# First layer's attention as seven staged steps in a written order, with TensorE turning the context's probabilities

## The chip, the cores and the metric

The kernel runs on one core of a Trainium2 chip. The metric is the device time of one execution in microseconds (us): lower is better. A profile is one more execution with the hardware profiler on. TensorE is called PE, VectorE DVE, ScalarE ACT, GpSimd POOL; SP is the engine that issues most DMAs.

## The reference, cut to what matters

Two layers over 2048 latent and 256 context tokens of width 1024. The change lies in the first layer's mixer: windowed attention with 16 query heads in 4 key/value groups, head size 64. A block of 128 latent queries reads its own and the two neighbouring key blocks (masked to a distance of 128) and all 256 context keys, in one softmax that also has a learned sink logit per head. The two context blocks read context keys only. The output is gated and projected.

```python
s_loc = jnp.where(valid, einsum('bqhgd,bkhd->bhgqk', qs, ks) * scale, NEG_INF)
s_ctx = einsum('bqhgd,bkhd->bhgqk', qs, kc) * scale
p = softmax(concatenate([s_loc, s_ctx, sink], axis=-1))
o = einsum('bhgqk,bkhd->bqhgd', p[..., :n_loc], vs) + einsum(..., p[..., n_loc:-1], vc)
y = (o * silu(g)) @ w_o
```

All products are done to about fp32 accuracy by splitting one factor into a high and a low half and adding matmuls.

## The kernel before

Three phases: the first layer's projections (to about 711 us), its attention with the output projection (711 to about 1450 us), and the second layer, which for most of its time is attention too (its dense part from about 1850 us).

The first layer's attention works in 72 units: 18 blocks of 128 tokens by 4 key/value groups, 4 heads each. Units 0 to 7 are context (256 keys), 8 to 11 and 68 to 71 are the outer latent blocks (512 keys), the 56 between have 640 keys and are called wide here. The steps of a unit:

- `score` (L509 to L523): PE makes a head's windowed scores (bank `pS`), DVE adds the mask, takes the maximum and moves them to SBUF (L513); the context scores of two heads share a bank and leave it by two more DVE operations (L523).
- `maxima` (L531 to L538): DVE makes the exponent's bias `nm` out of both maxima and the sink; `expo` (L542): ACT's four exps; `sums` (L547 to L549): the sink's exp, the sum, the reciprocal.
- `halves` (L558 to L562): ACT rounds the probabilities to fp16 (`hl`), POOL subtracts for the low half (L559), two heads at a time, and one DMA transposes all of it: 40 pieces of 128x128 in a wide unit.
- `value` (L573 to L595): ten matmuls into `pV`, the norms spread (`rb`, L579) and turned by PE (L581), the two halves of `pV` brought together by DVE (L585, L589), the gate on POOL (L590), and the split for the output projection (ACT L594, DVE L595).
- `project` (L616 to L623): the output projection in 16 parts per block of tokens, three matmuls of 512 columns each, drawn from the list `rest`.

Tile's scheduler sets the order on every engine from priorities here. The second layer's attention stands in a written order (`manual_schedule`), one `step` per 128 queries of a head: 6 of 18 key blocks are turned by PE (`turn`, L1125), ACT and DVE make their halves (L1132, L1134), and 12 pieces are rounded by ACT (L1113), subtracted by POOL (L1115) and transposed by two DMAs of 12 pieces each.

Of the kernel before, what the change touches and what calls it, by code (L numbers as in the profile page):

```python
# [19 lines left out]
KT = 8  # L20
# [12 lines left out]
def body(ctx: ExitStack, tc: tile.TileContext, x, c, ctxt, c_ctx, norm_g_0, ada_w_0, ada_b_0,  # L33
# [407 lines left out]
    work_2 = mk("a2k", 2)  # L441
    pss_2 = mk("a2ps", 4, space=PSUM)
# [9 lines left out]
    msk = w0p_2.tile([128, 640], F32, name="msk", tag="msk")  # L452
    dma(out=msk, in_=mask)
    vals = {}

    def load_v(t):

        raw = late2_2.tile([128, 4, 64], F32, name="vraw", tag="vraw", bufs=2)
        dma(out=raw.rearrange("p h d -> p (h d)"), in_=vv_d[t])
        if t < NC_:  # L460
            dst = late2_2.tile([128, 4, 128], F16, name=f"vc{t}", tag=f"vc{t}", bufs=1)
        else:
            dst = late2_2.tile([128, 4, 128], F16, name="vt", tag="vt", bufs=6)
# [3 lines left out]
        vals[t] = dst  # L467
# [10 lines left out]
    def load_unit(u):  # L478
# [10 lines left out]
        u["mx"] = small_2.tile([128, 4, 2], F32, name="mx", tag="mx")  # L489
        u["s"] = [None] * 4  # L490
# [4 lines left out]
    def load_gate(u):  # L495
        kv, t = u["kv"], u["t"]
        u["gt"] = late2_2.tile([128, 2, 128], F32, name="gt", tag="gt", bufs=2)
        dma(out=u["gt"], in_=ga_d[t // 3][:, 2 * kv:2 * kv + 2, (t % 3) * 128:(t % 3 + 1) * 128])

    def score(u, g):  # L500
        nw, nk, kv, wt = u["nw"], u["nk"], u["kv"], u["wt"]
        q2, mx = u["q2"], u["mx"]
        if g % 2 == 0:
            u["sp", g // 2] = work_2.tile([128, 2, 640], F32, name="s4", tag="s4", bufs=5)
        s = u["s"][g] = u["sp", g // 2][:, g % 2]
        if nw:
# [3 lines left out]
            PE.matmul(p[:, 0:nw], q2[:, g, :], kw[:, 1, 0:nw], start=False, stop=True)  # L510
            m0 = (wt[0] - u["t"] + 1) * 128
            assert all((wt[i] - u["t"] + 1) % 3 == (m0 // 128 + i) % 3 for i in range(len(wt)))
            V.tensor_tensor_reduce(out=s[:, 0:nw], in0=p[:, 0:nw], in1=msk[:, m0:m0 + nw], op0=ALU.add, op1=ALU.max,  # L513
                                   scale=1.0, scalar=-3e38, accum_out=mx[:, g, 0:1])
        if g % 2:
            p = pss_2.tile([128, 2, 256], F32, name="pS", tag="pS")
            for w in range(2):
                gw = g - 1 + w
                PE.matmul(p[:, w], q2[:, gw, :], kc[:, kv, 0, :], start=True, stop=False)
                PE.matmul(p[:, w], q2[:, gw, :], kc[:, kv, 1, :], start=False, stop=True)  # L520
            for w in range(2):
                gw = g - 1 + w
                V.tensor_scalar(out=u["sp", g // 2][:, w, nw:nk], in0=p[:, w], scalar1=1.0, scalar2=None,  # L523
                                op0=ALU.mult, op1=ALU.max, accum_out=mx[:, gw, 1:2])

    def maxima(u):
        hs = slice(u["kv"] * 4, u["kv"] * 4 + 4)
        mx = u["mx"]
        u["nm"] = nm = small_2.tile([128, 4], F32, name="nm", tag="nm")
        if u["nw"]:  # L530
            V.tensor_tensor(out=nm, in0=mx[:, :, 0], in1=mx[:, :, 1], op=ALU.max)  # L531
            V.tensor_tensor(out=nm, in0=nm, in1=sink8[:, hs], op=ALU.max)
        else:
            V.tensor_tensor(out=nm, in0=mx[:, :, 1], in1=sink8[:, hs], op=ALU.max)
        V.tensor_scalar(out=nm, in0=nm, scalar1=-0.125, scalar2=PS, op0=ALU.mult, op1=ALU.add)  # L535
        u["sm"] = small_2.tile([128, 4], F32, name="sm", tag="sm")
        u["es"] = es_ = small_2.tile([128, 4], F32, name="es", tag="es")
        V.tensor_tensor(out=es_, in0=sink[:, hs], in1=nm, op=ALU.add)  # L538

    def expo(u, g):  # L540
        nk, s = u["nk"], u["s"][g]
        A.activation(out=s[:, 0:nk], in_=s[:, 0:nk], func=AF.Exp, bias=u["nm"][:, g:g + 1],  # L542
                     scale=0.125, accum_out=u["sm"][:, g:g + 1])

    def sums(u):
        sm, es_ = u["sm"], u["es"]
        A.activation(out=es_, in_=es_, func=AF.Exp)  # L547
        V.tensor_tensor(out=sm, in0=sm, in1=es_, op=ALU.add)
        V.reciprocal(out=sm, in_=sm)  # L549

    def halves(u):

        nh = u["nk"]
        hl = mid_2.tile([128, 4 * 2 * 640], F16, name="hl", tag="hl")[:, 0:8 * nh]
        h4 = hl.rearrange("p (g w k) -> p g w k", g=4, w=2)
        for w in range(2):
            gs = slice(2 * w, 2 * w + 2)
            A.copy(out=h4[:, gs, 0], in_=u["sp", w][:, :, 0:nh])  # L558
            G.tensor_tensor(out=h4[:, gs, 1], in0=u["sp", w][:, :, 0:nh], in1=h4[:, gs, 0], op=ALU.subtract)  # L559
        n = nh // 128  # L560
        ht = mid_2.tile([128, 4 * 2 * 5, 128], F16, name="ht", tag="ht")[:, 0:8 * n]
        nc.sync.dma_start_transpose(out=ht, in_=hl)  # L562
        u["ht"] = ht.rearrange("p (g w k) q -> p g w k q", g=4, w=2)

    def value(u, i):
        wt, kv, t = u["wt"], u["kv"], u["t"]
        n = len(wt) + 2
        if i == 0:
            u["acc"] = psv_2.tile([128, 512], F32, name="pV", tag="pV")
        acc = u["acc"]  # L570
        vs = vals[(wt + [0, 1])[i]][:, kv, :]
        ph, pl = [u["ht"][:, :, w, i, :] for w in range(2)]
        PE.matmul(acc, vs, ph, start=(i == 0), stop=False)  # L573
        PE.matmul(acc, vs, pl, start=False, stop=(i == n - 1))
# [26 lines left out]
    def project(t):  # L601
# [3 lines left out]
        def part(nh, k):  # L605
# [18 lines left out]
            if nh == 1:  # L624
                dma(out=x1_d[t], in_=xt)
# [10 lines left out]
    NE = 2  # L636

    def stage(n, i):

        us = units[n] if n < nu else None  # L640
        ue = units[n - 1] if 0 < n <= nu else None
        ux = units[n - 2] if 1 < n <= nu + 1 else None
        uv = units[n - 3] if n > 2 else None
        if i == 0 and n + 1 < nu:
            load_unit(units[n + 1])
        if i == 0 and 2 <= n < nu + 2:
            load_gate(units[n - 2])
        nv = len(uv["wt"]) + 2 if uv else 0
        if ux and i == 0:
            sums(ux)  # L650
            halves(ux)
        if us and i < 4:
            score(us, i)
        if ue and i < 4:
            expo(ue, i)
        if uv and 1 <= i <= nv:
            value(uv, i - 1)
        if us and i == 4:
            maxima(us)
        if rest and 1 <= i <= 4 and (n > 6 or i < 3):  # L660
            with tc.high_priority(offset=-200):
                rest.pop(0)()
        if uv and i == 5:
            uv.clear()

    load_unit(units[0])
# [816 lines left out]
```

## Time and profile before

| what | us |
|---|---|
| three runs | 3612.79, 3618.59, 3619.69 (median 3618.59) |
| profiled execution, its own time | 3625.8 |
| span of that execution in the trace | 3623.9 |
| PE, DVE busy in the span | 3310.2, 2570.0 |
| granted TensorE clock, mean over the span | 0.959 of 2.4 GHz |

Busy times are of the whole span; the stretch in which the change lies has to be looked at by itself. The granted clock is a mean over its two levels, 1.2 and 2.4 GHz. PE's busy time includes the modelled tails of its matmuls, so what a matmul costs is read from one start to the next.

### The profile page before, as it was taken

To read this page: it belongs to the slowest core of one execution; us is meant where nothing else is said; L and a number is where in the kernel's file an instruction comes from. 1 tells how busy PE (TensorE), PEld (TensorE's weight loads), DVE (VectorE), ACT (ScalarE), POOL (GpSimd) and SP (SyncE) were. 2 spreads that over 40 slices of the span, in tenths; PEclk is the share of its full clock that TensorE was granted. 3 is DMA by queue.
4 is the path that set the end of the run, shared out by engine and by line. 5 is a ranking of instruction groups with operands and counts; after the bars stand their busy time and mean duration, and the time that the engine had idled before them with its cause. 6 is when DMAs were issued, how large, how long until landed. Compare 5 with 4: busy or idle time off the path is not lost. (4 is left out here: it accounts for less than half of the span.)

```text
span 3623.9 us, 58845 instructions
## 1 busy us (share of the span) xinstructions
PE 3310.2 (91%) x20044; PEld 2756.0 (76%) x20044; DVE 2570.0 (71%) x6964; ACT 2083.4 (57%) x3216; POOL 1945.2 (54%) x1403
## 2 busy tenths in 40 slices
PE   7868987878788888899999999999999999999999
PEld 5868987855555555899988888788777878787777
DVE  7544542399999998544368888788878788887655
ACT  6101300355555665544368888788878887888612
POOL 5433433166666666211147666766676666677622
PEclk9989988989989999899999999999999999999999
DMA  7444334489999999433368999989898989999943
GB/s 251 134 139 154 107 119 156 136 197 198 204 186 202 203 207 213 138 96 96 95 133 149 153 152 153 157 151 156 145 168 149 156 146 159 152 162 180 175 132 117
DMA packets 1391369, 568.76 MB, mean 157 GB/s; under 512 B 1168270, under 2 KB 1345342, under 8 KB 1390938
## 3 DMA queue, kind: packets, MB, share of 16 engines
q1 hardware_dynamic: 1308576, 501.76, 68.5%
q10 hardware_dynamic: 82492, 63.24, 7.6%
q8 instruction: 158, 2.59, 0.3%
q14 instruction: 143, 1.17, 0.1%
HBM read 180.18 MB, written 87.92 MB: 74 GB/s over the span
## 5 line engine op out<-in xcount | busy, mean ns | idle before, releaser
L1115 POOL TENSOR_TENSOR hl<-s,hl 128x1536 f16<-128x1536 f32 x256 | 798.4, 3119 | 494.1 <-ACT hl L1113 433.0
L1106 ACT ACTIVATE s<-s,m 128x2304 f32<-128x2304 f32 x256 | 569.3, 2224 | 147.3 <-DVE m L1097 126.5
L1148 PE MATMUL pV<-pT,vt 128*128 128x256 f16 x4608 | 636.9, 275 | 4.7 <-DVE ox L1161 4.5
L1091 DVE TENSOR_SCALAR_CACHE_REDUCE s<-pS 128x512 f32<-128x512 f32 (+1 forms) x768 | 458.6, 600 | 136.7 <-PE pS L1086 116.9
L1148 PEld LDWEIGHTS <-vt 128*128 128x128 f16 x4608 | 394.9, 98 | 180.6 <-issue 121.7
L559 POOL TENSOR_TENSOR hl<-s,hl 128x1280 f16<-128x1280 f32 (+2 forms) x144 | 349.5, 2445 | 157.9 <-ACT hl L558 155.7
L1113 ACT CAST hl<-s 128x1536 f16<-128x1536 f32 x256 | 377.0, 1473 | 51.2 <-DMA pT<-hl 29.7
L1091 DVE TENSOR_SCALAR_CACHE_REDUCE s<-pA 128x1024 f32<-128x1024 f32 x256 | 313.0, 1223 | 120.6 <-PE pA L1086 116.4
L542 ACT ACTIVATE s<-s,nm 128x640 f32<-128x640 f32 (+2 forms) x288 | 221.5, 771 | 259.6 <-DVE nm L535 259.6
L319 PE MATMUL pm<-hH,wH 128*128 128x384 f32 x864 | 304.5, 354 | 42.6 <-DVE rt L333 24.3
L1084 PE MATMUL pS<-kT,qH 96*128 96x512 f32 (+1 forms) x768 | 315.7, 411 | 1.3 <-DVE s L1091 1.1
L321 PE MATMUL pm<-hH,wL 128*128 128x384 f32 x864 | 301.4, 352 | 10.1 <-POOL wL L93 10.1
L320 PE MATMUL pm<-hL,wH 128*128 128x384 f32 x864 | 301.8, 352 | 0.7 <-DVE hL L273 0.7
L1134 DVE TENSOR_TENSOR pT<-pt,pT 128x384 f16<-128x384 f32 x512 | 261.8, 553 | 19.4 <-ACT pT L1132 19.4
L1085 PE MATMUL pS<-kT,qH 96*128 96x512 f32 (+1 forms) x768 | 274.0, 357 | 0.0
L1086 PE MATMUL pS<-kT,qL 96*128 96x512 f32 (+1 forms) x768 | 273.2, 356 | 0.0
L1084 PE MATMUL pA<-kT,qH 96*128 96x512 f32 x512 | 222.2, 434 | 0.0
L1132 ACT CAST pT<-pt 128x384 f16<-128x384 f32 x512 | 218.3, 477 | 1.4 <-PE pt L1125 0.6
L1125 PE MATMUL pt<-ident,s 128*128 128x128 f32 x1536 | 209.8, 273 | 0.0
L319 PEld LDWEIGHTS pm<-hH,wH 128*128 128x128 f32 x864 | 172.0, 200 | 48.2 <-DVE rt L333 24.0
L1086 PE MATMUL pA<-kT,qL 96*128 96x512 f32 x512 | 201.7, 394 | 0.2 <-POOL qL L1067 0.2
L1085 PE MATMUL pA<-kT,qH 96*128 96x512 f32 x512 | 201.2, 393 | 0.0
(320 smaller groups left out, 8553.7 us busy)
## 6 DMA issues: line engine op xcount, KB each, us to landing
wraw<-in_a_w_in_dram SPq DMA_DIRECT2D x80, 256.0 KB
q<-q2d ACTq DMA_DIRECT2D x72, 256.0 KB
xt<-in_x_dram SPq DMA_DIRECT2D x32, 512.0 KB
adw<-in_ada_w_dram SPq DMA_DIRECT2D x64, 256.0 KB
xt<-x1d SPq DMA_DIRECT2D x30, 512.0 KB
qf<-qbd ACTq DMA_DIRECT2D x128, 96.0 KB
q2d<-qH SPq DMA_DIRECT2D x48, 192.0 KB
q2d<-qL SPq DMA_DIRECT2D x48, 192.0 KB
```

What stands on the lines that cost most here:

```text
L319: PE.matmul(p[:, 0:384], wH[k][:, cs_], hH[:, k, :], start=(k == 0), stop=False)
L320: PE.matmul(p[:, 0:384], wH[k][:, cs_], hL[:, k, :], start=False, stop=False)
L321: PE.matmul(p[:, 0:384], wL[k][:, cs_], hH[:, k, :], start=False, stop=(k == KT - 1))
L559: G.tensor_tensor(out=h4[:, gs, 1], in0=u["sp", w][:, :, 0:nh], in1=h4[:, gs, 0], op=ALU.subtract)
L1084: PE.matmul(p, qH[:, bs], kH[:, ks], start=True, stop=False)
L1085: PE.matmul(p, qH[:, bs], kL[:, ks], start=False, stop=False)
L1086: PE.matmul(p, qL[:, bs], kH[:, ks], start=False, stop=True)
L1091: V.tensor_scalar(out=s[:, ks], in0=p, scalar1=1.0, scalar2=None, op0=ALU.mult, op1=ALU.max, accum_out=mx[:, i - 1:i])
L1106: A.activation(out=s, in_=s, func=AF.Exp, bias=u["m"], scale=SC, accum_out=sm[:, b % 4:b % 4 + 1])
L1113: A.copy(out=hl[:, 0], in_=s[:, NP0:T])
L1115: G.tensor_tensor(out=hl[:, 1], in0=s[:, NP0:T], in1=hl[:, 0], op=ALU.subtract)
L1148: PE.matmul(u["acc"], vts[h // 4, t][:, h % 4, :], u["pT"][:, :, t], start=(t == 0), stop=(t == NT - 1))
```

## The change

The first layer's attention now stands in a written order too, on all engines and SP's queue. A `stage(n)` holds steps of seven different units, n to n-6:

- Each head's context and windowed scores lie side by side in two banks, and one DVE operation moves all 640 columns to SBUF with mask and maximum (`score`, L522). `pS` has 2 buffers of two banks in place of 4 of one.
- The sink is a column of the scores (POOL writes it, `sinks`) and of the maxima; exp and sum cover it. `sums` is gone; `maxima` is one reduction (L527) and the scaling (L528).
- PE turns the context's two key blocks of each head (`turn`, 8 transposes a unit, L560), ACT copies the high half (L562), DVE subtracts for the low half one stage on (`turned`, L567). Only the window's keys go through `hl` and the DMA transposes: 24 pieces in place of 40, as two DMAs of 12 (L548, L550).
- The spread of the norms (L585) and the copy of the lower half of `pV` (L597) move from DVE to ACT, the low half of the gated output (L616) from DVE to POOL.
- `pT` (the turned context and the turned norms) has 2 buffers in place of 1, `pV` 1 in place of 2. Stores of finished blocks are issued a stage later; the splits of `w_o` have stages 1 to 8; two stages that ran inside the last input projection now run behind it.

```diff
+    def sinks(u):
+        u["s"] = work_2.tile([128, 4, 641], F32, name="s4", tag="s4")
+        for o in (u["s"][:, :, u["nk"]:u["nk"] + 1], u["mx"][:, :, 1:2]):
+            G.tensor_copy(out=o, in_=sink8[:, hs].unsqueeze(2))
...
     def score(u, g):
+        p = pss_2.tile([128, 1024], F32, name="pS", tag="pS")
+        PE.matmul(p[:, C:512], q2[:, g, :], kc[:, kv, 0, :], start=True, stop=False)
+        PE.matmul(p[:, C:512], q2[:, g, :], kc[:, kv, 1, :], start=False, stop=True)
...
+            PE.matmul(p[:, 512:512 + nw], q2[:, g, :], kw[:, 0, 0:nw], start=True, stop=False)
+            PE.matmul(p[:, 512:512 + nw], q2[:, g, :], kw[:, 1, 0:nw], start=False, stop=True)
...
+        V.tensor_tensor_reduce(out=u["s"][:, g, 0:nk], in0=p[:, C:C + nk], in1=msk[:, r, 0:nk], op0=ALU.add, op1=ALU.max,
+                               scale=1.0, scalar=-3e38, accum_out=u["mx"][:, g, 0:1])
...
     def maxima(u):
-            V.tensor_tensor(out=nm, in0=mx[:, :, 0], in1=mx[:, :, 1], op=ALU.max)
-            V.tensor_tensor(out=nm, in0=nm, in1=sink8[:, hs], op=ALU.max)
+        V.tensor_reduce(out=nm, in_=u["mx"], axis=AX.X, op=ALU.max)
         V.tensor_scalar(out=nm, in0=nm, scalar1=-0.125, scalar2=PS, op0=ALU.mult, op1=ALU.add)
-        V.tensor_tensor(out=es_, in0=sink[:, hs], in1=nm, op=ALU.add)
...
+        A.copy(out=h4[:, 0], in_=s[:, :, C:C + nw])
+        nc.sync.dma_start_transpose(out=hd[:, 0:n], in_=hl[:, 0:4 * nw])
+        G.tensor_tensor(out=h4[:, 1], in0=s[:, :, C:C + nw], in1=h4[:, 0], op=ALU.subtract)
+        nc.sync.dma_start_transpose(out=hd[:, n:2 * n], in_=hl[:, 4 * nw:8 * nw])
+
+    def turn(u):
...
+                    PE.transpose(out=p[:, g, k], in_=u["s"][:, 2 * r + g, k * 128:(k + 1) * 128], identity=ident)
+            A.copy(out=u["hp"][:, 0, 2 * r:2 * r + 2], in_=p)
+
+    def turned(u):
+            V.tensor_tensor(out=pl, in0=u["pt"][r], in1=ph, op=ALU.subtract)
...
+        us, ue, ut, uv = [at_0(n - d) for d in range(4)]
+        ua, ug, up = [at_0(n - d) for d in (4, 5, 6)]
...
+            sinks(us); gated(ug); split_o(up, 1); lower(ua); expo(ue)
+            turned(uv); norms(uv)
+            score(us, 0)
+            norms_2(ua); join(ua)
+        parts(1)
+            score(us, 1)
+            halves(ue)
+            turn(ut)
+        parts(1)
+            value(uv, 0)
+            score(us, 2)
+            value(uv, 1)
+        parts(1)
+            split_o(ug, 0)
+            score(us, 3)
+            maxima(us)
+            value(uv, 2)
+        parts(1 if len(rest) < 24 else 2)
+            value(uv, 3); value(uv, 4)
```

(The tests for units that do not exist yet are left out of `stage`, and short calls are drawn together.)

How this moves instructions, at two places of a wide unit. First DVE, at the end of a unit's maxima and the start of the next work. Before:

```order
L548 TENSOR_TENSOR sm<-sm,es 128x4
L513 ISA s_9713,mx<-pS,msk 128x384
L513 ISA mx 128x1
L465 SCALAR_TENSOR_TENSOR vt<-vraw,vsc,vt 128x4x64
L549 RECIPROCAL sm<-sm 128x4
L583 SCALAR_TENSOR_TENSOR gt<-pT,vinv,gt 128x256
L523 TENSOR_SCALAR s_9713,mx<-pS 128x256 x2
L531 TENSOR_TENSOR nm<-mx 128x4
L532 TENSOR_TENSOR nm<-nm,sink_5736 128x4
L595 TENSOR_TENSOR ogL<-u,ogH 128x256
L535 TENSOR_SCALAR nm<-nm 128x4
```

And now:

```order
L527 TENSOR_REDUCE nm<-mx 128x4
L528 TENSOR_SCALAR nm<-nm 128x4
L643 TENSOR_TENSOR y<-py,gate 128x512
L567 TENSOR_TENSOR hp<-pT,hp 128x512 x2
L583 RECIPROCAL sm<-sm 128x4
L522 ISA s_9761,mx<-pS,msk 128x640
L522 ISA mx 128x1
L593 SCALAR_TENSOR_TENSOR gt<-pT,vinv,gt 128x256
L603 TENSOR_TENSOR u<-pV,tl 64x256 x2
```

Of the operations that read nothing from PSUM, L548, L531, L532 and L595 are gone from DVE; L528 (L535 before) stays as it was, and the subtractions for the turned context (L567) stand behind it. Every second stage `y` of the projection (L643) stands between them.

Second PE, at the start of a stage. Before, around the turned norms (L581):

```order
L509 MATMUL pS<-kw_5732,q_9871 128x384
L510 MATMUL pS<-kw_5732,q_9871 128x384
L519 MATMUL pS<-kc,q_9871 128x256
L520 MATMUL pS<-kc,q_9871 128x256
L519 MATMUL pS<-kc,q_9871 128x256
L520 MATMUL pS<-kc,q_9871 128x256
L581 MATMUL pT<-ident,rb 128x128 x2
L618 MATMUL py<-woH,ogL 128x512
```

And now, from the second half of a unit's first head on:

```order
L518 MATMUL pS<-kw_5729,q_9959 128x384
L519 MATMUL pS<-kw_5729,q_9959 128x384
L592 MATMUL pT<-ident,rb 128x128 x2
L637 MATMUL py<-woH,ogH 128x512
L638 MATMUL py<-woL,ogH 128x512
L639 MATMUL py<-woH,ogL 128x512
L513 MATMUL pS<-kc,q_9959 128x256
L514 MATMUL pS<-kc,q_9959 128x256
L518 MATMUL pS<-kw_5729,q_9959 128x384
L519 MATMUL pS<-kw_5729,q_9959 128x384
L560 MATMUL pT<-ident,s_9861 128x128 x8
L637 MATMUL py<-woH,ogH 128x512
```

The turned norms (L592) now take one of the two `pT` buffers that the eight turned pieces (L560) use as well, in rotation.

## Rows read from the trace of the kernel before

**Rows 1.** Stretches: us; busy us (instructions) of PE, PEld, DVE, ACT, POOL; granted clock, DMA share, GB/s.

```profile
711.00:801.00 90.00, 62.96 (x276) 43.75 (x275) 76.44 (x238) 52.34 (x132) 58.45 (x41) 0.81 0.87 211
801.00:1392.00 591.00, 482.41 (x2219) 334.85 (x2219) 569.24 (x1600) 342.69 (x681) 372.09 (x196) 0.93 1.01 201
1422.00:1500.00 78.00, 62.95 (x300) 50.64 (x299) 55.52 (x134) 46.79 (x91) 32.23 (x27) 0.83 0.66 191
2000.00:3200.00 1200.00, 1188.55 (x7934) 964.36 (x7933) 963.55 (x2742) 973.18 (x1184) 820.85 (x495) 1.00 0.93 154
```

**Rows 2.** Timeline of DVE: start us, us, line; bias of units 12, 68, 71.

```profile
800.66 0.17 DVE L535 TENSOR_SCALAR nm<-nm 128x4 f32<-128x4 f32 x1
...
1392.48 0.17 DVE L535 TENSOR_SCALAR nm<-nm 128x4 f32<-128x4 f32 x1
...
1422.06 1.25 DVE L535 TENSOR_SCALAR nm<-nm 128x4 f32<-128x4 f32 x1
```

**Rows 3.** Groups by line, 801 to 1392 us: count | busy us, mean ns | idle before.

```profile
L542 ACT ACTIVATE s<-s,nm 128x640 f32<-128x640 f32 x224 | 183.0, 818 | 228.0 <-DVE nm L535 228.0
...
L532 DVE TENSOR_TENSOR nm<-nm,sink 128x4 f32<-128x4 f32 x55 | 55.0, 1001 | 0.6
L595 DVE TENSOR_TENSOR ogL<-u,ogH 128x256 fp32r<-128x256 f32 x56 | 54.6, 974 | 5.1 <-ACT ogH L594 5.0
...
L531 DVE TENSOR_TENSOR nm<-mx 128x4 f32<-128x4 f32 x55 | 42.2, 767 | 0.2
...
L535 DVE TENSOR_SCALAR nm<-nm 128x4 f32<-128x4 f32 x55 | 35.2, 639 | 0.7
```

**Rows 4.** Timeline of all engines, DVE and POOL beside each other.

```profile
1003.85 5.22 POOL L559 TENSOR_TENSOR hl<-s,hl 128x1280 f16<-128x1280 f32 x2
...
1004.02 2.46 DVE L548 TENSOR_TENSOR sm<-sm,es 128x4 f32<-128x4 f32 x1
...
1007.18 1.91 DVE L532 TENSOR_TENSOR nm<-nm,sink 128x4 f32<-128x4 f32 x1
```

**Rows 5.** Two lines each by itself: duration ns min/median/max, first and last start.

```profile
L535 DVE TENSOR_SCALAR nm<-nm x72: 139/170/2607, 678.1 to 1422.1; 128x4 f32<-128x4 f32 x72
...
L1097 DVE TENSOR_SCALAR m<-m x256: 147/153/156, 1850.1 to 3411.2; 128x1 f32<-128x1 f32 x128
```

**Rows 6.** Timeline of PE in the first layer's attention, at the full clock.

```profile
1010.54 0.28 PE L519 MATMUL pS<-kc,q 128*128 128x256 f32 x1
1010.66 0.28 PE L520 MATMUL pS<-kc,q 128*128 128x256 f32 x1
...
1011.67 0.34 PE L510 MATMUL pS<-kw,q 128*128 128x384 f32 x1
1011.84 0.39 PE L618 MATMUL py<-woH,ogL 128*128 128x512 f32 x1
1012.07 0.40 PE L616 MATMUL py<-woH,ogH 128*128 128x512 f32 x1
...
1013.56 0.38 PE L573 MATMUL pV<-ht,vt 128*128 128x512 f16 x1
1013.78 0.38 PE L574 MATMUL pV<-ht,vt 128*128 128x512 f16 x1
```

**Rows 7.** Timeline of PE in the second layer's attention, the turned pieces.

```profile
2505.54 0.82 PE L1125 MATMUL pt<-ident,s 128*128 128x128 f32 x6
2506.12 0.48 PE L1084 MATMUL pS<-kT,qH 96*128 96x512 f32 x1
```

**Rows 8.** Groups by line, 2000 to 3200 us, the second layer's halves.

```profile
L1115 POOL TENSOR_TENSOR hl<-s,hl 128x1536 f16<-128x1536 f32 x195 | 608.0, 3118 | 376.7 <-ACT hl L1113 323.2 <-DVE s L1091 49.6 <-ACT pT L1132 1.9
...
L1113 ACT CAST hl<-s 128x1536 f16<-128x1536 f32 x194 | 285.7, 1473 | 32.0 <-DMA pT<-hl 20.8
...
L1134 DVE TENSOR_TENSOR pT<-pt,pT 128x384 f16<-128x384 f32 x390 | 199.4, 553 | 8.4 <-ACT pT L1132 8.4
...
L1132 ACT CAST pT<-pt 128x384 f16<-128x384 f32 x389 | 166.0, 477 | 0.7
```

More of the change, by code (lines that the diff above doesn't have):

```diff
@@ L510, in score @@
[L510 to L524, printed above, removed]
+            PE.matmul(p[:, 512:512 + nw], q2[:, g, :], kw[:, 0, 0:nw], start=True, stop=False)
@@ L565, in value @@
     def value(u, i):
-        wt, kv, t = u["wt"], u["kv"], u["t"]
+        wt, kv = u["wt"], u["kv"]
         n = len(wt) + 2
+        if i >= n:
+            return
         if i == 0:
             u["acc"] = psv_2.tile([128, 512], F32, name="pV", tag="pV")
[L570 to L574, printed above, removed]
@@ L591, in value, with norms @@
-        if kv == 0:
+        vs = vals[([0, 1] + wt)[i]][:, kv, :]
+        for w in range(2):
+            PE.matmul(u["acc"], vs, u["hp"][:, w, :, i, :] if i < 2 else u["hd"][:, w, :, i - 2, :],
+                      start=(i == 0 and w == 0), stop=(i == n - 1 and w == 1))
+    def norms(u):
+        V.reciprocal(out=u["sm"], in_=u["sm"])
+        rb = late2_2.tile([128, 4, 64], F32, name="rb", tag="rb", bufs=1)
+        A.copy(out=rb, in_=u["sm"].unsqueeze(2).broadcast_to([128, 4, 64]))
+        u["rb"] = rb
@@ new lines, in join, with gated, split_o @@
+    def join(u):
+        ah = u["acc"][0:64, :].rearrange("p (j w q) -> p j w q", w=2, q=128)
+        u["o"] = late2_2.tile([128, 2, 128], F32, name="u", tag="u", bufs=3)
+        for w in range(2):
+            V.tensor_tensor(out=u["o"][64 * w:64 * w + 64], in0=ah[:, :, w, :], in1=u["tl"][:, :, w, :], op=ALU.add)
+    def gated(u):
+        G.tensor_tensor(out=u["o"], in0=u["o"], in1=u["gt"], op=ALU.mult)
+    def split_o(u, w):
+        kv, t = u["kv"], u["t"]
+        if kv == 0 and w == 0:
@@ L635, in body, with at_0 @@
     nu = len(units)
[L636 to L644, printed above, removed]
-            load_unit(units[n + 1])
[L646 to L658, printed above, removed]
-            maxima(us)
[L660 to L664, printed above, removed]
+    def at_0(n):
+        return units[n] if 0 <= n < nu else None
@@ new lines, in stage, with parts @@
+    def stage(n):
+        us, ue, ut, uv = [at_0(n - d) for d in range(4)]
+        ua, ug, up = [at_0(n - d) for d in (4, 5, 6)]
+        def parts(m):
+            for _ in range(m if n > 8 else 0):
+                if rest:
+                    rest.pop(0)()
+        todo_, stores[:] = stores[:], []
+        if n + 1 < nu:
+            load_unit(units[n + 1])
+        if ut:
+            load_gate(ut)
+        for f in todo_:
+            f()
+        if n < KT:
+            wo_load(n)
+        if 0 < n <= KT:
+            wo_split(n - 1)
+        for j in [j for j, r in ready.items() if r <= n]:
+            ready.pop(j)
+            split_v(j)
+        for j in raws:
+            ready.setdefault(j, n + 2)
+        if us:
+            sinks(us)
+        if ug:
+            gated(ug)
+        if up:
+            split_o(up, 1)
+        if ua:
+            lower(ua)
+        if ue:
+            expo(ue)
+        if uv:
+            turned(uv)
+            norms(uv)
+        if us:
+            score(us, 0)
+        if ua:
+            norms_2(ua)
+            join(ua)
+        parts(1)
+        if us:
+            score(us, 1)
+        if ue:
+            halves(ue)
+        if ut:
+            turn(ut)
+        parts(1)
+        if uv:
+            value(uv, 0)
+        if us:
+            score(us, 2)
+        if uv:
+            value(uv, 1)
+        parts(1)
+        if ug:
+            split_o(ug, 0)
+        if us:
+            score(us, 3)
+            maxima(us)
+        if uv:
+            value(uv, 2)
+        parts(1 if len(rest) < 24 else 2)
+        if uv:
+            value(uv, 3)
+            value(uv, 4)
@@ L668, in body @@
     load_v(1)
-    run([f for g in range(3, 6) for f in project_in(4, g)], [lambda n=n, i=i: stage(n, i) for n in range(NE) for i in range(6)])
+    for j in list(raws):
+        split_v(j)
+    run([f for g in range(3, 6) for f in project_in(4, g)])
     close(psm_1, hp_1, x_1, wp_1)
+    work_2 = mk("a2k", 3)
     mid_2 = mk("a2m", 2)
```

156 lines of the change are left out of this document (78 added, 78 removed).

## The prediction

> **What bounds the kernel now.** The stretch first: the change touches only the first layer's attention, so I cut the span there, and within it take the 56 wide units, from the bias of unit 12 to that of unit 68 on DVE [rows 2]: (1392.48 - 800.66) / 56 = 10.57 us a unit. In that stretch the windows show DVE busy for 569 of 591 us, 96%, PE for 482, ACT for 343 and POOL for 372 [rows 1]. DVE is the bound; the idle time of the others is the consequence: ACT's exps stand idle for 228 us, all of it behind the bias from L535 [rows 3].
>
> Then: what fills DVE? Three operations on 128x4 numbers, L531, L532 and L535, have means of 767, 1001 and 639 ns, the split L595 974 ns [rows 3]. The same form of L535 takes 170 ns in its median and 2607 at most [rows 5]. The timeline says what happens in the long ones: POOL's two subtractions fill 5.22 us from 1003.85 to 1009.07; DVE's L548 starts at 1004.02 and ends at 1006.48, about when the first of the two does, L532 starts at 1007.18 and ends at 1009.09, with the second [rows 4]. They wait for POOL's running instruction to end. The Trainium skill ("SBUF — State Buffer", section "Who interferes with whom") has a rule for it: a DVE operation that needs both read ports and a POOL operation shut each other out for a whole instruction, whoever issued first. The trace agrees, with 2.46 and 1.91 us beside it, and adds that a scaling of a single column is never held: 153 ns median, 156 at most [rows 5].
>
> What this costs a unit: L531, L532 and L535 together 2.41 us where three times 0.17 would do, 1.90 lost; L595 0.97, where its 256 columns would be 0.37 by L1134's 553 ns for 384 [rows 8], 0.60 lost. With L548, which has one wait of 2.46 shown, some 3 us of 10.57.
>
> DMA is the second suspect: its share is 1.01 in the same stretch [rows 1]. Forty pieces of 128x128 go through it per unit.
>
> **The change, part by part.** *DVE.* L531, L532, L548 and L595 leave it, with their waits; also L579, L589. What is left, priced high by L1134's 1.44 ns a column: four moves of 640 columns at 0.92, two subtractions of 512 (L567) at 0.74, four small ones at 0.17, the spread of the norms 0.37, the join 0.74, half a `y` 0.37: 7.3 us. Columns are overpriced that way, since 553 ns holds a fixed part too; taking 0.75 a move (estimate: a fixed part of about 0.1 taken off) it is 6.3. One operation can still be held, L528, the old L535.
>
> *PE.* By starts of neighbours [rows 6]: 256 columns 0.12, 384 0.17, 512 0.23 in f32 and 0.22 in f16. A wide unit: 8 x 0.12 + 8 x 0.17 + 10 x 0.22 (value) + 12 x 0.23 (four parts) = 7.28. New are eight transposes beside the two of the norms. The second layer's six take 2506.12 - 2505.54 = 0.58, or 0.097 each [rows 7]: ten 0.97, sum **8.25 us** a stage at the full clock. So PE becomes the engine with the most work, and nothing of DVE's gain below 8.25 counts.
>
> Here a rule speaks against the change. The Trainium skill ("TensorE: Matmul & The Clock Gate", "Part 4: PE-mode transpose") gives about 275 ns for such a transpose inside a kernel, and says that transposes do not count as work towards the full clock; by its price the stage would be 8.25 + 10 x 0.178 = 10.03 us and nearly all of the gain gone. The trace of the second layer, where six transposes stand in every step, disagrees: 0.097 each, and a granted clock of 1.00 over 1200 us [rows 1, 7].
>
> *ACT and POOL.* ACT: four exps of 0.82 [rows 3], the rounding of 1536 columns 1.47 [rows 8], two copies of 512 at about 0.6 (from L1132's 477 for 384 [rows 8]), the lower half 0.6, the norms' spread and a split about 0.35 each: near 7.3. POOL: one subtraction of 3.12 [rows 8] in place of two that end 5.22 apart [rows 4], the gate, and the low split: below 6. Neither bounds.
>
> *DMA and SP.* 24 pieces a unit, in two DMAs of 12, in place of 40. The second layer moves 24 pieces in 1200 / 195 = 6.15 us (195 subtractions, [rows 8]) at a share of 0.93 [rows 1] with PE full, so a stage above 8 us leaves DMA room. On SP the second transpose waits for POOL's subtraction, and the loads of keys stand behind it; those are first used two stages on, some 9 us later. I cost this at nothing; without that slack the keys would be late.
>
> *The wait that the change brings.* L528 comes at the end of a stage while POOL's subtraction may run; it is held until that ends. Behind it on DVE stand the subtractions L567, behind those a `pT` buffer (two buffers, three uses a stage), and for that buffer PE waits with the turned norms (L592), which stand 0.6 us into the next stage, with everything of PE behind them. When does POOL end? From a stage's start: lower half 0.6, four exps 3.3, spread 0.35, rounding 1.47, POOL 3.12, hand-overs 0.3: 9.1. Then L567's first half, 0.69: 9.9. PE would reach L592 at 8.25 + 0.6 = 8.85 without it. So a wait of up to about 1.0 us a stage, with `y` ahead of L567 every second stage up to 0.6 more. It does not hit in full each time: a stage that started late moves its own chain less than PE's. Ends: 8.25 (never) and 10.1 (each time, with `y` and a clock a little below full). I take **9.2** for a stage, the middle, since chain and PE come within 1 us of each other and neither clearly leads.
>
> *Sum, on the profiled execution.* Wide units: 56 x (10.57 - 9.2) = 76.7 us less. Units 68 to 71: three intervals from 1392.48 to 1422.06, 29.6 us [rows 2], now about 8.2 each (512 keys): 5 less. Before the wide units stand 90 us at 63 of PE work [rows 1]: eight context stages need no DMA transposes and cost PE some 5.6 (8 x 0.12, 10 x 0.097, 4 x 0.22, 12 x 0.23), 45 together, four outer ones 8 each, 32; but two stages lose their place beside the last projection, some 10. Eighty-seven against 90: I take 0, with 10 either way. The end: 1422 to 1500 has PE at 63 of 78 us [rows 1], and a pipeline of seven stages drains through half-empty ones: 2 us more in three of them, 6 (0 to 12). Net 77 + 5 - 6 = 76 less: 3625.8 - 76 = 3550. The profiled execution's own time lies 7.2 us above the median of the runs, so for runs: **3543**.
>
> **The rivals.** *No stall* (L528 finds POOL idle, or PE never waits for L592): a stage of 8.25; 56 x 2.32 = 130, with 5 more and 6 less as above 129: 3490 in runs. For it: PE full in the second layer [rows 1]; against it: chain 9.9 against 8.85.
>
> *PE dearer than its rows*: transposes that stand among matmuls of another kind cost more than six in a row, or their inputs come late. At a stage of 10.2: 56 x 0.37 = 21 less, with the rest 20: 3598. For it: nothing in rows 7. The price of the Trainium skill's page named above leads to 10.03 and the same place.
>
> *A change without effect*: DVE's waits go elsewhere (say the chain ACT, POOL, DVE sets 10.5 a stage): 56 x 0.07 = 4 less, with the rest 3: 3616. For it: a DVE that has 6.3 to 7.3 of work and one wait of up to 2.6 [rows 5] comes to 9.9 at most, so it needs a second wait.
>
> *Slower: the clock.* Where PE waited, the granted clock was 0.81 (711 to 801) and 0.83 (1422 to 1500), against 1.00 where it was full [rows 1]. A written order makes every wait of PE stop all of PE. Stage work of 8.25 becomes 10.57 at a mean clock of 0.78: from there the change costs time. At 0.75 it is 11.0: 56 x 0.43 = 24 more, with the rest 25: 3644. Against it: PE would be busy for 8.25 of about 9.2, 90%, more than the 482 of 591 (82%) that stood at 0.93 [rows 1].
>
> **How the numbers follow.** Forecast (stages of 8.7 to 9.9, so 3515 to 3582) 0.62; no stall 0.13; PE dearer 0.10; no effect 0.05; slower by the clock 0.10. The range takes in the forecast's own with the 10 either way of the start, half of no stall (its upper half, by that same 10), and PE dearer: 3498 to 3600, some 0.78 of the cases. A measurement of this kernel can tell about 0.2%, 7 us: faster is forecast, no stall and PE dearer, 0.85; same 0.05; slower 0.10.
>
> **What the profile after would show.** Right: from one unit's first score to the next 9.2 us on PE; DVE busy below 75% of the stretch; L528 up to 3 us long, just while POOL's one subtraction runs; PE waiting at L592 for DVE's L567; DMA's share below 0.9; ACT no longer idle 228 us behind the bias; clock above 0.95; ten transposes within about 1 us. Wrong: PE waiting at scores (L513) for DVE's moves, at value for a DMA, or for keys; transposes at over 0.2 us each; clock below 0.85 in the wide units.

## The result, and the profile after

The changed kernel takes 3531.19 us (median of 4 runs, 3526.57 to 3537.91) against 3615.69 of before (4 runs): ratio 0.9768, interval 0.9754 to 0.9783, 84.5 us less. 3543 was forecast, 3498 to 3600 the range. The profiled executions differ by a little more, 3623.9 - 3529.2 = 94.7 us of span, since that of before took 3625.8 us, 10 above the median of its runs.

The windows of the changed kernel, for the stretches that answer to [rows 1]: to the bias of unit 12, the wide units, the end, the second layer. Columns as there.

```profile
711.00:790.00 79.00, 60.91 (x314) 48.55 (x315) 56.16 (x164) 57.94 (x145) 37.87 (x49) 0.83 0.53 146
790.00:1298.00 508.00, 476.52 (x2680) 352.32 (x2679) 385.44 (x936) 391.21 (x796) 296.81 (x308) 1.00 0.81 178
1324.00:1402.00 78.00, 64.03 (x342) 52.14 (x341) 57.89 (x131) 50.10 (x100) 35.16 (x34) 0.93 0.65 199
1900.00:3100.00 1200.00, 1187.51 (x7915) 964.00 (x7914) 961.71 (x2733) 971.57 (x1183) 819.66 (x495) 1.00 0.92 153
```

The wide units last 508 us in place of 591. PE is busy for 476.5 of them, 94%, DVE for 76% where it had 96%; the granted clock is 1.00 (0.93 before), DMA's share 0.81 (1.01).

DVE's timeline, the bias of the same three units as in [rows 2]:

```profile
789.93 0.17 DVE L528 TENSOR_SCALAR nm<-nm 128x4 f32<-128x4 f32 x1
...
1298.73 1.67 DVE L528 TENSOR_SCALAR nm<-nm 128x4 f32<-128x4 f32 x1
...
1324.64 0.31 DVE L528 TENSOR_SCALAR nm<-nm 128x4 f32<-128x4 f32 x1
```

A stage takes (1298.73 - 789.93) / 56 = 9.09 us in place of 10.57. Split by these rows, the 94.7 us are: 83.0 in the 56 wide units, 3.7 in units 68 to 71 (29.6 to 25.9), 10.7 before unit 12 (800.66 to 789.93), and 2.7 given back after unit 71.

Bias to bias, stages take 8.44, 9.56, 8.44 and 10.02 us in turn (medians). What the long ones wait for is seen in the timeline of all engines, here the end of one stage and the start of the next (rows between left out):

```profile
1005.59 3.02 POOL L549 TENSOR_TENSOR wraw<-s,wraw 128x1536 f16<-128x1536 f32 x1 [4.89 <-ACT wraw L547]
...
1007.53 1.10 DVE L528 TENSOR_SCALAR nm<-nm 128x4 f32<-128x4 f32 x1
...
1008.03 0.47 PE L513 MATMUL pS<-kc,q 128*128 128x256 f32 x1
...
1008.34 0.28 PE L514 MATMUL pS<-kc,q 128*128 128x256 f32 x1
...
1008.55 0.68 DVE L643 TENSOR_TENSOR y<-py,gate 128x512 f32<-128x512 f32 x1
...
1009.15 0.47 DVE L469 SCALAR_TENSOR_TENSOR vt<-vraw,vsc,vt 128x256 f16<-128x256 f32 x1
...
1009.54 1.28 DVE L567 TENSOR_TENSOR hp<-pT,hp 128x512 f16<-128x512 f32 x2
...
1010.37 0.41 PE L592 MATMUL pT<-ident,rb 128*128 128x128 f32 x2 [1.39 <-DVE hp L567]
```

POOL's subtraction ends at 1008.61 and the bias L528, begun at 1007.53, at 1008.63. Behind it stand `y` and, in every fourth stage, the split of the values (L469); then the subtractions L567, the first of which frees the `pT` buffer that PE's L592 takes. PE waits 1.39 us. In the stages without `y`, POOL's subtraction has ended before L528 starts. L528 takes 0.17 to 0.22 us in half of them and 0.41 to 0.66 in the other half, until POOL's gate product (L606) ends:

```profile
944.27 0.73 POOL L606 TENSOR_TENSOR u<-u,gt 128x256 f32<-128x256 f32 x1
...
944.58 0.44 DVE L528 TENSOR_SCALAR nm<-nm 128x4 f32<-128x4 f32 x1
```

There L592 follows at once, and the stage takes PE's own 8.43. So the long hold and `y` fall into the same stages.

PE's groups by line in the wide units, and its timeline at a turn:

```profile
L560 PE MATMUL pT<-ident,s 128*128 128x128 f32 x448 | 58.0, 272 | 0.0
L592 PE MATMUL pT<-ident,rb 128*128 128x128 f32 x112 | 22.6, 283 | 31.0 <-DVE hp L567 30.9
```

```profile
1001.88 1.03 PE L560 MATMUL pT<-ident,s 128*128 128x128 f32 x8
1002.67 0.48 PE L637 MATMUL py<-woH,ogH 128*128 128x512 f32 x1
```

PE's idle time at L592, 31.0 us over 56 stages, is the only idle time of matmuls worth a line. The 31.0 us are 0.55 a stage; the stage loses 9.09 - 8.43 = 0.66, since PE's busy time covers the start of each wait with the tail of the matmul before. Eight transposes take 1002.67 - 1001.88 = 0.79 us, 0.099 each; their recorded durations, 272 ns in the mean, overlap.

### The profile page after: what moved, and what is told of

It reads as the page before. It is cut to its first block, busy times and chain, and to the rows that moved or that the text cites. A ratio compares the mean times of both kernels' runs of the same rounds, so it can differ in the third digit from the quotient of the medians.

```text
span 3529.2 us, 59672 instructions
## 1 busy us (share of the span) xinstructions
PE 3309.9 (94%) x20620; PEld 2785.7 (79%) x20620; DVE 2347.7 (67%) x6173; ACT 2137.8 (61%) x3348; POOL 1850.8 (52%) x1539
## 5 line engine op out<-in xcount | busy, mean ns | idle before, releaser
L522 DVE CUSTOM_DVE_ANT_0 s<-pS,msk 128x640 f32<-128x640 f32 (+2 forms) x288 | 218.0, 759 | 191.1 <-PE pS L519 127.7
L549 POOL TENSOR_TENSOR wraw<-s,wraw 128x1536 f16<-128x1536 f32 (+1 forms) x64 | 186.0, 2906 | 216.8 <-ACT wraw L547 216.8
L534 ACT ACTIVATE s<-s,nm 128x641 f32<-128x641 f32 (+2 forms) x288 | 221.8, 774 | 13.0 <-DVE nm L528 12.9
L1162 PE MATMUL pA<-kT,qH 96*128 96x512 f32 x512 | 221.7, 433 | 0.0
```

Source lines behind the costliest of these rows:

```text
L1162: PE.matmul(p, qH[:, bs], kH[:, ks], start=True, stop=False)
```

## The experiments

Twelve kernels. Times are medians; ratios with the interval are to runs of the kernel before that were taken beside each (medians of 3613.87 to 3617.89). The diffs are cut to the lines that matter; `...` stands for lines left out. A unit is the time from the bias of unit 12 to that of unit 68, over 56; the shares are PE's and DVE's busy time between the two, and the granted clock and DMA's share are of the same stretch.

| kernel | us | ratio | unit us | PE, DVE busy | clock | DMA |
|---|---|---|---|---|---|---|
| before | 3615.69 | 1 | 10.57 | 82%, 96% | 0.93 | 1.01 |
| changed | 3531.19 | 0.9768 (0.9754-0.9783) | 9.09 | 94%, 76% | 1.00 | 0.81 |
| 1 norms later | 3557.86 | 0.9835 (0.9821-0.9849) | 9.47 | 91%, 70% | 1.00 | 0.78 |
| 2 columns | 3500.86 | 0.9683 (0.9664-0.9702) | 8.76 | 97%, 75% | 1.00 | 0.86 |
| 3 before, DVE relieved | 3647.75 | 1.0089 (1.0066-1.0112) | 11.13 | 81%, 71% | 0.88 | 0.92 |
| 4 before, DMA relieved | 3639.35 | 1.0063 (1.0048-1.0078) | 11.01 | 81%, 95% | 0.91 | 0.66 |
| 5 changed, Tile's order | 3500.41 | 0.9690 (0.9664-0.9715) | 8.95 | 97%, 78% | 0.99 | 0.83 |
| 6 changed, more DMA | 3544.69 | 0.9813 (0.9790-0.9837) | 9.42 | 92%, 72% | 0.99 | 1.14 |
| 7 before, one reduction | 3605.53 | 0.9977 (0.9962-0.9993) | 10.62 | 83%, 94% | 0.92 | 0.99 |
| 8 no wait | 3489.57 | 0.9661 (0.9641-0.9681) | 8.58 | 100%, 76% | 1.00 | 0.87 |
| 9 before, halves of 24 | 3551.84 | 0.9817 (0.9800-0.9834) | 9.56 | 89%, 93% | 0.95 | 0.75 |
| 10 both 3 and 9 | 3517.69 | 0.9719 (0.9696-0.9742) | 9.07 | 90%, 85% | 0.97 | 0.84 |
| 11 Tile's order, columns | 3471.04 | 0.9596 (0.9578-0.9613) | 8.60 | 99%, 76% | 1.00 | 0.89 |
| 12 drain in Tile's order | 3485.54 | 0.9630 (0.9611-0.9648) | 8.58 | 100%, 76% | 1.00 | 0.87 |

### The wait in the changed kernel (1, 2, 8)

**1, norms later.**

```diff
         if ua:
-            norms_2(ua)
             join(ua)
         parts(1)
             score(us, 1)
+            norms_2(ua)
             halves(ue)
-            turn(ut)
         parts(1)
+            turn(ut)
```

> The changed kernel with the turned norms one head later on TensorE (behind the second head's scores), the context's turn behind one more part of the projection, and the join ahead of the norms. Theory A (a stage is 8.44 us of TensorE's work, and every second one waits up to 1.4 us for a pT buffer that DVE's subtraction of the turned context frees late): that wait goes, stages come to 8.4 to 8.6, 56 times about 0.55 less, so 3495 to 3505 us. Rival B (the chain over ScalarE, GpSimd and DVE sets the pace, the buffer is only where it shows): the wait moves to the turn, to the scores or to the values, stages stay at 9.0 to 9.1, 3525 to 3535.

Both were wrong: 27 us slower than the changed kernel. The place is that of B, the turn. PE's groups by line from 860 to 1300 us:

```profile
L560 PE MATMUL pT<-ident,s 128*128 128x128 f32 x375 | 58.9, 279 | 39.3 <-DVE gt L593 39.3
...
L592 PE MATMUL pT<-ident,rb 128*128 128x128 f32 x92 | 17.5, 272 | 0.0
```

L592 no longer waits, but the next user of its buffer does: the turn needs it back from DVE's L593, which now stands behind the second head's move. With two buffers and three uses a stage the wait was handed on, and made longer. It does not show that the chain over ScalarE and GpSimd sets the pace; the next two runs show that it doesn't, since PE's busy share goes to 97% and 100% in them.

**2, columns.**

```diff
-        V.tensor_scalar(out=nm, in0=nm, scalar1=-0.125, scalar2=PS, ...)
+        for g in range(4):
+            V.tensor_scalar(out=nm[:, g:g + 1], in0=nm[:, g:g + 1], scalar1=-0.125, scalar2=PS, ...)
```

> The changed kernel with the scaling of the maxima as four operations of one column each. Theory A (the scaling of 128x4 is held while GpSimd subtracts, a column is not): each column takes 0.15 us whatever GpSimd does, 0.6 in place of 1.1 us, the wait for the pT buffer shrinks by about 0.5 in every second stage, 56 times 0.25 less: 3515 to 3521 us. Rival B (the wait is not the scaling's, but that of the projection's product and the value split that stand behind it): no change, or 4 times 0.15 more than 0.17 where it wasn't held: 3529 to 3545.

A, and more than it: 30 us. The line by itself, changed kernel and this one:

```profile
L528 DVE TENSOR_SCALAR nm<-nm x72: 170/465/1972, 702.6 to 1324.6; 128x4 f32<-128x4 f32 x72
```

```profile
L529 DVE TENSOR_SCALAR nm<-nm x288: 142/144/154, 707.7 to 1307.7; 128x1 f32<-128x1 f32 x144
```

No column is ever held. Four of them start 0.06 us apart and are through in 0.33 us, not the 0.6 that I had put; so the long stages lose about 0.74 each (10.02 to 9.30, 9.56 to 8.82). The two profiled executions are 24.7 us apart, and the wide units give 56 x 0.33 = 18 of these. Another 7.5 lie after unit 71, where nothing was edited: that stretch took 2186.5 to 2204.5 us in the traces of all these kernels, the changed kernel's being the longest, and I have no cause for its spread.

**8, no wait.** Besides the columns:

```diff
     def turned(u):
         for r in range(2):
+            if r == 1:
+                for f in late_y: f()    # y and its addition to xt
             V.tensor_tensor(out=pl, in0=u["pt"][r], in1=ph, op=ALU.subtract)
...
             score(us, 0); norms_2(ua); join(ua)
+            split_v(j)    # from the start of the stage
-        parts(1)
             score(us, 1)
+        parts(1)
```

> The changed kernel with the scaling in single columns, the projection's product y and the split of the values moved off the way to the turned context's first subtraction (y between its two halves, the split behind the join), and the first part of the projection behind the second head's scores. Theory A (the stages above 8.44 us are the wait for the pT buffer, in which y is 0.68 and the split 0.47): every stage 8.4 to 8.6, 56 times 0.3 less than with columns alone: 3480 to 3490. Rival B (another wait takes its place: the projection's for y, the turn's for the gate): stages of 8.7 to 8.9 as with columns alone, 3495 to 3505.

A. Its windows:

```profile
786.00:1265.00 479.00, 478.18 (x2677) 351.48 (x2676) 362.96 (x1100) 391.33 (x798) 292.48 (x305) 1.00 0.87 189
```

PE is busy for 478 of 479 us, and the wait at the turned norms is gone. So hold, product and split were that wait. Of the 0.66 us a stage 0.51 went, and 0.15 are left (8.58 against 8.43): every second stage still takes 8.68 to 8.78. There the turn takes 943.28 - 942.27 = 1.01 us in place of 951.83 - 951.04 = 0.79:

```profile
942.27 1.26 PE L561 MATMUL pT<-ident,s 128*128 128x128 f32 x8
943.28 0.48 PE L642 MATMUL py<-woH,ogH 128*128 128x512 f32 x1
...
951.04 1.03 PE L561 MATMUL pT<-ident,s 128*128 128x128 f32 x8
951.83 0.48 PE L642 MATMUL py<-woH,ogH 128*128 128x512 f32 x1
```

The waits between 786 and 1265 us name what its weight loads wait for:

```profile
PEld pT L561 <- DVE gt L598: 7.5, 28, 0.5
```

It is the turn's wait for the gate (L598, L593 of the changed kernel), which B had named, in 28 of 56 stages; the tails of the matmuls hide it in PE's busy share.

### Which part of the change brings the gain (3 to 7, 9, 10)

**3, before with DVE relieved.**

```diff
-        V.tensor_copy(out=rb, in_=u["sm"].unsqueeze(2)...)
+        A.copy(out=rb, in_=u["sm"].unsqueeze(2)...)
-        V.tensor_copy(out=tl, in_=acc[64:128, :]...)
+        A.copy(out=tl, in_=acc[64:128, :]...)
-        V.tensor_tensor(out=ogL, in0=o, in1=ogH.bitcast(F32), op=ALU.subtract)
+        G.tensor_tensor(out=ogL, in0=o, in1=ogH.bitcast(F32), op=ALU.subtract)
```

> The kernel before with three DVE operations moved and nothing else: the norms' spread and the copy of the lower half to ScalarE, the low half of the gated output to GpSimd, 2.24 us of DVE's 10.2 a unit. Theory A (before, DVE was the bound, with the waits for GpSimd in it): units of 9 to 9.8 us, 3530 to 3575. Rival C (DMA at a share of 1.01 was a bound beside it, 40 pieces a unit): units stay above 10.3, 3600 to 3617.

Slower than before by 30 us, which neither had (C's unit above 10.3 came, its time did not). The waits in the wide units, longest first (engine, line, what it waited for: us in total, times, longest):

```profile
POOL hl L559 <- ACT hl L558: 83.8, 45, 6.7
PEld pS L509 <- DVE mx L513: 79.1, 59, 5.6
POOL u L590 <- DVE u L589: 77.5, 25, 7.5
ACT s L542 <- DVE nm L535: 73.2, 25, 5.3
ACT hl L558 <- DMA ht<-hl: 64.2, 27, 6.6
DVE gt L583 <- DMA gt<-gad: 59.9, 27, 4.7
```

DVE fell from 96% to 71%, and no other engine filled: each waits for another, two of the six lines for a DMA (the transposes 64 us, the gate 60). Taking 2.2 us of work off the busiest engine bought nothing. The moves put that work on ACT and POOL, and the granted clock was lower too (0.88 for 0.93); the run does not separate these.

**4, before with DMA relieved.**

```diff
-        nc.sync.dma_start_transpose(out=ht, in_=hl)
+        m = min(n, 3)
+        nc.sync.dma_start_transpose(out=ht[:, 0:8 * m], in_=hl[:, 0:8 * m * 128])
...
-        ph, pl = [u["ht"][:, :, w, i, :] for w in range(2)]
+        ph, pl = [u["ht"][:, :, w, min(i, 2), :] for w in range(2)]
```

> The kernel before with only 24 of a unit's 40 pieces transposed (the values then use some pieces twice, so the output is not the reference's): DMA's work is that of the changed kernel, everything else stays. Theory A (DVE is the bound): within 10 us of before, 3600 to 3625, units 10.4 to 10.6. Rival C (DMA is): units of 9.5 to 10.2, 3555 to 3595.

C falls: DMA's share went from 1.01 to 0.66 and the unit from 10.57 to 11.01. DVE stayed at 95%. That it came out 22 us slower is beyond A too; no cause is shown (the granted clock was 0.91 for 0.93).

**5, the changed kernel in Tile's order.**

```diff
-    with tc.manual_schedule(engines=ORDERED | {ET.SP}):
+    if True:
         for n in range(nu + 7):
```

> The changed kernel with all its operations and buffers, but the order of the first layer's attention left to Tile's scheduler. Theory A (the operations carry the gain: less on DVE, fewer of its operations held): within 15 us of the changed kernel, 3520 to 3550. Rival D (after the first four runs: relief of one engine doesn't shorten a unit while the scheduler's order lets engines wait on each other; the written order carries the gain): units of 9.8 or more, 3570 to 3660.

D falls, and A was too careful: 31 us faster than in the written order. Of the 29.6 us between the profiled executions, though, the wide units give only 56 x 0.13 = 7.4, and 18.0 lie after unit 71, the stretch whose spread has no cause yet. That the operations and buffers carry the gain is shown; that Tile's order is better by 31 us is not. Here the hold of L528 shows at the exps (the waits, 790 to 1260 us):

```profile
ACT s L534 <- DVE nm L528: 56.7, 36, 3.0
POOL wraw L549 <- ACT wraw L547: 52.6, 36, 4.4
```

PE goes on with other work in the meantime; its share is 97%.

**6, more DMA.** 16 pieces more a wide unit, 8 behind each transpose, into a place that nothing reads.

```diff
         nc.sync.dma_start_transpose(out=hd[:, 0:n], in_=hl[:, 0:4 * nw])
+        nc.sync.dma_start_transpose(out=x[0], in_=hl[:, 0:1024])
```

> The changed kernel with 16 more pieces of each wide unit transposed by DMA into a place that nothing reads, behind each of the two transposes 8: DMA's work as before, 40 pieces. Theory A (with 40 pieces DMA is busy for 10.7 us a unit, 1.01 of 10.57; so without the turn on TensorE the ordered kernel would be bound by DMA): stages of 10.2 to 10.9, 3590 to 3635. Rival E (the share overstates it, DMA has room): stages below 9.4, 3531 to 3550.

E, though at its edge: 13.5 us, stages of 9.42. The share went to 1.14, and the stage stayed far below 10.2: a share of 1 is not a full DMA. What PE waits for now is the keys (waits in the wide units; 0.5 us in all in the changed kernel):

```profile
PE pS L518 <- DMA kw<-kkd: 25.3, 21, 3.7
```

The keys stand behind the transposes in SP's queue, where a transpose takes some 1.4 to 1.8 us to issue, and with four a stage the queue has hardly a gap:

```profile
848.78 1.40 SPq L552 DMA_TRANSPOSE hd<-wraw  x1
850.27 1.71 SPq L553 DMA_TRANSPOSE wraw<-wraw  x1
852.03 0.59 SPq L41 DMA_DIRECT2D kw<-kkd  x1
```

That the queue and not the transfer itself makes them late is read from these rows; no run separates the two.

**7, before with one reduction.**

```diff
-            V.tensor_tensor(out=nm, in0=mx[:, :, 0], in1=mx[:, :, 1], op=ALU.max)
-            V.tensor_tensor(out=nm, in0=nm, in1=sink8[:, hs], op=ALU.max)
+        V.tensor_reduce(out=nm, in_=mx, axis=AX.X, op=ALU.max)    # mx[:, :, 2] is the sink, from GpSimd
-        V.tensor_scalar(out=nm, in0=nm, ...)
+        for g in range(4): V.tensor_scalar(out=nm[:, g:g + 1], in0=nm[:, g:g + 1], ...)
```

> The kernel before with one part of the change alone: the sink as a column of the maxima (written by GpSimd) and one reduction in place of two maxima of two inputs, and the scaling as four single columns. 2.41 us of DVE's 10.2 a unit become about 0.5, nothing is moved to ScalarE. Theory A (DVE, with the waits for GpSimd in it, was what bound a unit): units of 8.9 to 9.6, 3530 to 3570. Rival D (the scheduler's order: what DVE no longer waits for, it waits for elsewhere): units above 10.2, 3595 to 3650.

D in the unit, 10.62, and 0.23% faster as a whole. DVE's groups in the wide units say where 1.9 us went; first before, then this run (L593, L577 and L546 are L595, L579 and L548 of before):

```profile
L579 DVE COPY rb<-sm 128x256 f32<-128x256 f32 x56 | 32.2, 574 | 0.2
L548 DVE TENSOR_TENSOR sm<-sm,es 128x4 f32<-128x4 f32 x56 | 29.2, 522 | 2.8 <-ACT es L547 2.7
```

```profile
L593 DVE TENSOR_TENSOR ogL<-u,ogH 128x256 fp32r<-128x256 f32 x59 | 80.2, 1360 | 7.1 <-ACT ogH L592 7.1
L536 DVE TENSOR_TENSOR es<-sink,nm 128x4 f32<-128x4 f32 x56 | 48.2, 860 | 0.8
L577 DVE COPY rb<-sm 128x256 f32<-128x256 f32 x58 | 45.3, 780 | 2.0 <-PE pT L579 1.9
L546 DVE TENSOR_TENSOR sm<-sm,es 128x4 f32<-128x4 f32 x55 | 41.9, 763 | 4.0 <-ACT es L545 3.6 <-ACT s L540 0.4
```

The split L593 has a mean of 1360 ns, against 974 of L595 in [rows 3], the spread 780 against 574, the sum 763 against 522, and the sink's sum L536 860 against 352 (L538 before). DVE's instructions lost their work and DVE stayed at 94%: a hold that is taken from one operation falls on the next one that can be held.

**9, before with halves of 24 pieces.** The context's 16 pieces are neither rounded, nor subtracted, nor transposed; DVE's and TensorE's instructions are those of before.

```diff
-        nh = u["nk"]
+        nh = min(u["nk"], 384)
...
-        ph, pl = [u["ht"][:, :, w, i, :] for w in range(2)]
+        ph, pl = [u["ht"][:, :, w, min(i, 2), :] for w in range(2)]
```

> The kernel before with only 24 of a wide unit's 40 pieces rounded by ScalarE, subtracted by GpSimd and transposed by DMA (the values use some pieces twice, so the output is not the reference's); TensorE and DVE have the work of before. So GpSimd's two subtractions take about 3.1 us a unit in place of 5.2. Theory A, as the runs so far leave it (DVE is held for as long as GpSimd subtracts; a held operation that is taken away leaves its wait to the next one, but less subtracting means less waiting): units of 9.2 to 9.9, 3540 to 3585. Rival D (waits only move, whatever is relieved): units above 10.3, 3600 to 3640.

A: 9.56 a unit, 66 us. DVE's groups, the same instructions as in [rows 3]:

```profile
L595 DVE TENSOR_TENSOR ogL<-u,ogH 128x256 fp32r<-128x256 f32 x57 | 41.8, 733 | 4.5 <-ACT ogH L594 4.4
L532 DVE TENSOR_TENSOR nm<-nm,sink 128x4 f32<-128x4 f32 x56 | 31.5, 563 | 0.5
...
L531 DVE TENSOR_TENSOR nm<-mx 128x4 f32<-128x4 f32 x56 | 27.1, 483 | 0.2
L535 DVE TENSOR_SCALAR nm<-nm 128x4 f32<-128x4 f32 x55 | 24.0, 436 | 0.4
```

All four are shorter (733 for 974, 563 for 1001, 483 for 767, 436 for 639), with nothing of DVE edited. DVE's busy time is 497.1 / 56 = 8.9 us a unit where it was 569.2 / 56 = 10.2. By run 4 DMA's relief alone does nothing; of the other two engines, it is GpSimd's subtractions that DVE's operations end with [rows 4]. Their longest hold follows the length of one subtraction, which has a median of 2.63 us before and 1.65 here. L532 in both kernels, min/median/max:

```profile
L532 DVE TENSOR_TENSOR nm<-nm,sink x64: 131/164/2591, 768.6 to 1419.9; 128x4 f32<-128x4 f32 x64
```

```profile
L532 DVE TENSOR_TENSOR nm<-nm,sink x64: 135/164/1614, 766.3 to 1364.3; 128x4 f32<-128x4 f32 x64
```

So the shorter holds come from GpSimd. How much of the 1.0 us a unit is theirs, and how much is that rounding, subtraction and transposes follow one another faster, no run separates.

**10, both.** The edits of 9 and of 3 together.

> As the 24 pieces for ScalarE, GpSimd and DMA in the kernel before, and the three DVE operations moved too (norms' spread and lower half to ScalarE, low half of the gated output to GpSimd). Theory A (in the kernel before DVE on one side, and GpSimd's halves with the 40 transposes behind them on the other, both filled a unit; only both together shorten it): units of 8.3 to 9.2, 3480 to 3540. Rival D (the scheduler's order keeps engines waiting on each other): units above 10, 3585 to 3640.

A. The three moves that cost 30 us on the kernel before bring 34 once the halves are short. This kernel does without the turn on TensorE and its subtraction, so its 9.07 is not quite the changed kernel's 9.09, but it is the same size.

### The best of both (11, 12)

**11** is run 5 with the columns of run 2.

> The changed kernel with Tile's order and the scaling in single columns. Theory A (the held scaling delays the exps there too): units 0.2 to 0.6 shorter than 8.95, 3468 to 3490. Rival B (DVE has idle time in that order, the hold is hidden): 3495 to 3505.

A: 3471 us, the fastest here, 4.0% below before and 1.7% below the changed kernel. The exps' wait for the bias (the same view) is nearly gone:

```profile
ACT s L535 <- DVE nm L529: 10.5, 16, 1.6
```

**12** is run 8 with the written order only to the last unit's scores.

```diff
         for n in range(nu):
             stage(n)
+    if True:
+        for n in range(nu, nu + 7):
...
+            stage(n)
```

> The kernel without the wait (single columns, product and split moved, first part later), with the written order only up to the last unit's scores: the six stages behind it, in which the pipeline drains, are left to Tile's scheduler, which can draw the second layer's first work in between. Theory A (the drain in written order costs TensorE some 10 us of waits and clock): 3474 to 3482. Rival B (the drain is bound by its own chain): 3486 to 3494.

Nearer to B, 4 us less than run 8 with runs that overlap: undecided.

## Why the prediction was right

*A stage.* 9.2 was forecast, 9.09 measured, by the mechanism that was given: bias held by POOL's subtraction, L567 behind it, PE waiting for the `pT` buffer at L592, in turn with stages that don't wait. POOL ends 9.0 us after its stage's start (1008.61, where the next stage begins at 1008.03 and this one is 8.43 long); 9.1 had been added up. PE's own work is 8.43, not 8.25. Some first matmuls behind another kind take longer than the rows that I took (L513 to L514 above: 0.31, not 0.12; the four L637 of a stage 1.47, not 0.92), and the fp16 matmuls less (four in 0.69); the sum was off by 0.18. The mean wait is 9.09 - 8.43 = 0.66 us, not 0.95. The two misses have opposite signs, and 9.2 was taken as the middle of 8.25 and 10.1; that it came within 0.11 is in part luck. What I did not name is the split L469, 0.47 us in every fourth stage.

*The transposes.* 0.099 each by the trace, as taken from [rows 7]. The Trainium skill ("TensorE: Matmul & The Clock Gate", "Part 4: PE-mode transpose") gives about 275 ns; that is the mean duration of one here, 272 ns, but not what it costs among others. The clock stayed at 1.00 in the wide units.

*The other terms.* Wide units: 83.0 for 76.7. Units 68 to 71: 3.7 for 5. The start: 10.7 for 0, at the edge of the 10 either way that I had left; its cause stays open, and the bias of unit 12 falls anywhere from 790 to 805 us in the kernels that keep the order of before. The drain: 2.7 for 6, a hit or a miss by chance, since that stretch spreads by 18 us. Sum 94.7 for 76 on the profiled executions; by medians 84.5 for 76. The largest miss is the start. Of the signs that were named, DVE is busy for 76% where below 75 was said, and L528 takes 1.1 us at most in the wide units, since it starts late in POOL's 3.0.

*Rivals.* PE's clock did not fall, the turned pieces were not dear, and "no stall" is nearly what run 8 made: 8.58, where I had 8.25 and PE's own work is 8.43.

*Where the reading failed, though the number held.* "DVE is the bound", with DVE's work counted as so many instructions at their means: runs 3 and 7 took 2.2 and 1.9 us of it away and units did not get shorter. By these runs what bound the kernel before was DVE together with the making of the halves: DVE's small operations last until POOL's subtraction ends, so their means are POOL's time, and by run 7 they don't go away with the operations. It took shorter halves (the turn, run 9: 1.0 us a unit) and less on DVE (run 10: another 0.5). That it is POOL's time alone is argued: in run 3 DVE stood idle for 29% of longer units, so holds are not all of it, and run 9 shortens ACT's, POOL's and DMA's part at once, of which run 4 tests DMA's alone. The changed kernel has both, and its forecast was safe since it was made from PE's work and from one hold that was left. DMA, "the second suspect", was no bound by itself (runs 4 and 6).

*The written order* is not what made it faster (run 5). It makes each wait of PE stop all of PE, as the fourth rival feared; with the hold gone it still loses 0.16 us a unit to Tile's order (runs 2 and 11: 8.76 and 8.60), and nothing once product and split are off the way as well (run 8: 8.58).

Left open: why runs 3 and 4 are slower than before and not just level, what moved the start by 10.7 us, and what spreads the time after unit 71 by up to 18 us.

## What to carry to other kernels

An operation whose mean is several times its median may be a wait under another name, as L535 was here (639 against 170 ns): ask for whose end it lasts, and shorten that one, since taking the operation away can hand the wait to the next (run 7). A busy share of PE near 100% can still hide waits under the tails of its matmuls; compare starts, stage by stage (run 8). Before a written order is made for a group of engines, look which of its operations can be held, and what stands behind them on the same engine; here four single columns in place of one 128x4 were worth 0.33 us a stage of 9.09. A single edit that gains nothing (run 3) may still be half of one that does (run 10).

## What the runs showed of the hardware

- A scaling of 128x4 in SBUF took 0.17 to 1.97 us beside POOL's subtractions; four scalings of 128x1, 0.142 to 0.154 us each, begun 0.06 us apart, were never held, which makes them faster in the mean (0.33 against 0.69 us in the wide units).
- The longest hold of a 128x4 maximum (L532) went from 2.59 to 1.61 us when POOL's subtraction went from 2.63 to 1.65 us (medians; before and run 9).
- DMA's share can stand at 1.14 over 526 us: with 16 pieces more a unit the stage grew by 0.33 us only.
- An identity transpose of 128x128 f32 costs PE 0.099 us in a row of eight at the full clock, at a recorded duration of 0.27.
